# The modulation's sums over partitions: 192 products with a column of ones on TensorE in place of 192 transposes with ScalarE sums

## Chip, cores and metric

The kernel runs on one core of a Trainium2 chip. The metric is the device time of one execution in microseconds. A core has five engines that run side by side, each with a queue that it works through in order: TensorE (PE in the profile, its weight loads PEld), VectorE (DVE), ScalarE (ACT), GpSimd (POOL) and SyncE (SP), which here issues all transfers. Matrix products are written to PSUM, everything else lies in SBUF.

## What is computed

Two layers of a decoder trunk over 256 positions of width 2048, in f32. Each layer has a mixer (sliding-window attention beside RWKV-7 heads) and a SwiGLU FFN. Both are modulated by a vector `mod` that is computed from the condition `c`:

```python
cond = jax.nn.silu(c)                                       # (1, 2048)
for l in range(2):
    mod = (cond @ w_ada[l] + b_ada[l]).reshape(B, 6, 1, 2048)
    sh_m, sc_m, gt_m, sh_f, sc_f, gt_f = [mod[:, i] for i in range(6)]
    u = x * (1 + sc_m) + sh_m
    proj = u @ w_in[l]
    ...
    mix = jnp.concatenate([y_attn, y_rwkv], axis=-1) @ w_out[l]
    x = layer_norm(ALPHA * x + gt_m * mix, ln1_w[l], ln1_b[l])
    u = x * (1 + sc_f) + sh_f
    gate, up = jnp.split(u @ w_gate_up[l], 2, axis=-1)
    x = layer_norm(ALPHA * x + gt_f * ((silu(gate) * up) @ w_down[l]), ln2_w[l], ln2_b[l])
```

The change concerns `cond @ w_ada[l]`, a product of one row with a matrix of 2048 x 12288 in each layer, and of that its last step alone.

## The kernel before

**The weight stream.** The large products (`w_in`, `w_out`, `w_gate_up`, `w_down`) are taken with f32 weights split in two parts. Each piece of 128x1024 is loaded (`raw`), rounded on ScalarE (`hi`, line 380), the rest formed on DVE (`lo`, line 381), and TensorE multiplies three times: lines 402, 403 and 405 where the weights stream, lines 414 to 416 where they are the loaded operand. `raw`, `hi` and `lo` have 4, 3 and 2 buffers.

**The modulation** isn't computed on TensorE. A column of `w_ada` is 2048 long, 16 blocks of 128. For 1024 columns at a time (`ada_steps`, one such piece is called a unit here) 16 tiles `ast` are loaded, and DVE adds them up, each multiplied by its piece of `cond` (lines 255 and 257), into `aacc` (128x1024, one buffer). What is left is a sum over the 128 partitions for each of the 1024 columns: that is `ada_sums`. There are 20 units; they run beside the weight stream from the prologue's end to the second layer's mixer. In the prologue `ada_first` does the same for the first layer's shift and scale in five parts of 4, 4, 2, 4 and 2 blocks, twice each (lines 304 and 306).

**`ada_sums` before.** For each 128 columns TensorE transposes the block of `aacc` into a PSUM bank (line 277), four blocks to a bank. ScalarE copies each transposed block onto itself and adds up along the row with `accum_out` (line 281), which gives 128 sums, one to a partition, as one column of `asum` in SBUF. DVE adds the bias and writes `mods` (line 284). For gates (modulations 2 and 5) a further transpose and a copy bring the row to DRAM (lines 289 to 291).

**Banks.** `bank()` gives out two PSUM banks in turn, `m0` and `m1`, with one buffer each. In the prologue `turn` is set to 0, 0, and all its users (`ada_sums`, the transposes of x at line 354) share one bank: each waits until the one before has been read.

**Order.** The code is written as generators: `pump` and `adv` advance the units between steps of the stream. Then a scheduler orders each engine's instructions by a timeline of its own, so an edit can move instructions that it doesn't touch. On the engines the order is fixed: an instruction that waits holds up all behind it on its engine.

**Two other products** serve for comparison in the prediction. Line 647 sums squares over 64 columns (`kkn`) with two columns of `bones`; line 710 scales `bkc` with a diagonal matrix:

```python
PE.matmul(ssb[0:64, o:o + 2], lhsT=kkn[:, cc * CH:(cc + 1) * CH], rhs=bones[:, 0:P:64], ...)   # 647: 2 x 4 a group of heads
PE.matmul(kb[:, cc * P:(cc + 1) * P], lhsT=bkc[:, cc, :], rhs=s_["de"][:, cc, :], ...)         # 710: 2 x 3 a group of heads
```

There are four groups of heads in each of two layers. `lhsT` is the loaded operand, `rhs` the one that streams. Both are plain f32 products.

Of the kernel before, what the change touches and what calls it, by code (L numbers as in the profile page):

```python
# [10 lines left out]
F32 = mybir.dt.float32  # L11
F32R = mybir.dt.float32r
I32 = mybir.dt.int32
AF = mybir.ActivationFunctionType
ALU = mybir.AluOpType
AX = mybir.AxisListType
# [3 lines left out]
P = 128  # L20
# [24 lines left out]
PARTS = (4, 4, 2, 4, 2)  # L45
LAG = 2
WB = (4, 3, 2)
RED = 1
AR = (3, 7)
AA = (1, 45)  # L50
AP = (0.65, 0.3)
# [16 lines left out]
def hybrid_trunk_kernel(  # L68
# [8 lines left out]
    V, S, G, PE = nc.vector, nc.scalar, nc.gpsimd, nc.tensor  # L77
# [5 lines left out]
    adap = ctx.enter_context(tc.tile_pool(name="adap", bufs=1))  # L83
# [6 lines left out]
    def bank(name="mb", tag="mb"):  # L90

        if tag == "cb":
            return ps.tile([P, 512], F32, tag="cb", name=name)
        t = f"m{turn[0]}"
        turn[0] ^= turn[1]
        return ps.tile([P, 512], F32, tag=t, name=name, bufs=1)


    ident = const.tile([P, P], F32, name="ident")
# [40 lines left out]
    ones = const.tile([P, 1], F32, name="ones")  # L140
# [19 lines left out]
    def prm(l, nm, i, n=1):  # L160
        o = PC[nm] + i
        return par[l][:, o // P, o % P:o % P + n]
# [83 lines left out]
    def ada_steps(l, mod, c0):  # L246

        src = w_ada[l].rearrange("(j p) n -> p j n", p=P)
        n0 = mod * D + c0
        acc = adap.tile([P, 1024], F32, tag="aacc", name="aacc")  # L250
        for j in range(KT):
            t = adap.tile([P, 1024], F32, tag="ast", name="ast", bufs=2)
            dma(t, src[:, j, n0:n0 + 1024])
            if j == 0:
                V.tensor_scalar_mul(acc, t, cond[:, 0:1])
            else:
                ins = V.scalar_tensor_tensor(acc, t, cond[:, j:j + 1], acc, ALU.mult, ALU.add)  # L257
                if anchor:
                    tc.add_manual_dep(ins.ins, anchor[0], order, reason="behind the weight stream")
            yield  # L260
        for _ in range(LAG):
            yield

        ada_sums(l, mod, c0, [acc[:, i * P:(i + 1) * P] for i in range(8)])
        done.add((l, mod, c0 // 1024))
        yield

    def ada_sums(l, mod, c0, blocks):

        col = mod * KT + c0 // P  # L270
        n = len(blocks)
        sm = adap.tile([P, 8], F32, tag="asum", name="asum", bufs=2)
        for q in range(0, n, 4):
            b = bank()
            m = min(4, n - q)
            for i in range(m):
                PE.transpose(b[:, i * P:(i + 1) * P], blocks[q + i], ident)
            for i in range(m):
                bi = b[:, i * P:(i + 1) * P]
                if RED:  # L280
                    S.activation(bi, bi, AF.Copy, accum_out=sm[:, q + i:q + i + 1])
            if not RED:
                V.reduce_sum(sm[:, q:q + m], b[:, 0:m * P].rearrange("p (i k) -> p i k", k=P), axis=AX.X)
        V.scalar_tensor_tensor(mods[l][:, col:col + n], sm[:, 0:n], 1.0 if mod in (1, 4) else 0.0,
                               prm(l, "b_ada", col, n), ALU.add, ALU.add)
        if mod in (2, 5):
            row = adap.tile([8, P], F32, tag="arow", name="arow", bufs=2)[0:n]
            rb = bank()
            PE.transpose(rb[0:n, 0:P], mods[l][:, col:col + n], ident)
            S.copy(row, rb[0:n, 0:P])  # L290
            dma(gates[l, mod // 3, c0 // P:c0 // P + n], row)

    def ada_first(pool, c0, w):

        src = w_ada[0].rearrange("(j p) (m n) -> p j m n", p=P, m=6)
        acc = pool.tile([P, 2, 512], F32, tag="aacc", name="aacc", bufs=2)[:, :, 0:w]
        jj = 512 // w
        for j0 in range(0, KT, jj):
            t = pool.tile([P, jj, 2, w], F32, tag="ast", name="ast", bufs=8)
            for j in range(jj):  # L300
                dma(t[:, j], src[:, j0 + j, 0:2, c0:c0 + w])
            for j in range(jj):
                if j0 + j == 0:
                    V.tensor_scalar_mul(acc, t[:, j], cond[:, 0:1])
                else:
                    V.scalar_tensor_tensor(acc, t[:, j], cond[:, j0 + j:j0 + j + 1], acc, ALU.mult, ALU.add)
            yield
        for m in range(2):
            ada_sums(0, m, c0, [acc[:, m, i * P:(i + 1) * P] for i in range(w // P)])
# [1038 lines left out]
```

## Time and profile before

| | |
|---|---|
| median of 3 runs | 2715.88 us (2715.45 to 2717.28) |
| the profiled execution | 2716.41 us, its span 2714.6 us |
| mean granted TensorE clock | 0.96 |
| read from HBM | 622.08 MB, 234 GB/s over the span |
| aacc steps on DVE (line 257), 300 of 128x1024 | 388.7 us busy, 1296 ns each |
| weight splits on ACT and DVE (lines 380, 381), 728 each | 757.8 us and 885.9 us busy |
| transposes of aacc (line 277) | 192, 31.4 us busy |

Times are in microseconds from the span's start, unless marked ns. "Busy" is the time in which an engine had an instruction running; records of products overlap, so the spacing of their starts tells more than their lengths. In rows of waits stand the waiting instruction, what it waited for, the time in total, how often, and the longest. In rows of the timeline stand the start, the length of the whole group, the engine, the line, the operation, output and inputs, the shapes, and the count; in brackets the idle time of the engine before it and what ended it. The granted clock is TensorE's, 1.00 at full speed.

### The profile page before, as it was taken

The page shows a single profiled execution, that of the slowest core. Times are in us where ns is not written, and L with a number is a line of the kernel's source. Part 1 is how long each engine was busy: PE and PEld are TensorE (multiplying, and loading weights), DVE is VectorE, ACT ScalarE, POOL GpSimd, SP SyncE. Part 2 cuts the span into 40 slices and gives each one's busy share as a digit, 9 for nine tenths or more (in the row PEclk, how much of TensorE's full clock was granted, in tenths as well). Part 3 has the DMA queues.
Part 4 walks back from the last instruction along what each step waited for, and adds up shares of the span by engine and source line. Part 5 has one row for each costly group of instructions (what it writes and reads, how often), then busy time and mean ns, then how long its engine had stood idle before and what let it go on. Part 6 is the DMA issues. An engine that isn't in the chain of part 4 may idle for free. (4 is left out here: it accounts for less than half of the span.)

```text
span 2714.6 us, 41774 instructions
## 1 busy us (share of the span) xinstructions
PE 2517.3 (93%) x15325; PEld 2103.9 (78%) x15325; DVE 1853.5 (68%) x2437; ACT 1188.4 (44%) x2029; POOL 180.0 (7%) x387
## 2 busy tenths in 40 slices
PE   3789998797999999999999989989899999999998
PEld 2787886575788888888889877867788888888887
DVE  6877767879777777777788677565764545545456
ACT  2364452434444444444445544534444444344442
POOL 1002111003000000000000022110120000000000
PEclk9799997798999999999999999979999999999999
DMA  9968667597888888889888586423746655566654
GB/s 310 382 193 254 203 197 225 179 331 250 313 318 308 303 307 304 294 302 309 304 287 288 175 251 204 116 75 130 258 163 190 190 190 190 194 191 189 190 190 148
DMA packets 351999, 637.49 MB, mean 235 GB/s; under 512 B 75894, under 2 KB 142898, under 8 KB 350258
## 3 DMA queue, kind: packets, MB, share of 16 engines
q1 hardware_dynamic: 351794, 634.82, 71.1%
q8 instruction: 120, 1.97, 0.3%
q14 instruction: 85, 0.70, 0.1%
HBM read 622.08 MB, written 12.62 MB: 234 GB/s over the span
## 5 line engine op out<-in xcount | busy, mean ns | idle before, releaser
L380 ACT CAST hi<-raw 128x1024 fp32r<-128x1024 f32 (+2 forms) x728 | 757.8, 1044 | 1097.6 <-PE acc L405 810.6
L381 DVE TENSOR_TENSOR lo<-raw,hi 128x1024 fp32r<-128x1024 f32 (+2 forms) x728 | 885.9, 1220 | 515.8 <-PE acc L403 335.2
L403 PE MATMUL acc<-lo,u 128*128 128x512 f32 x1568 | 515.7, 396 | 16.9 <-DVE lo L381 16.6
L405 PE MATMUL acc<-hi,u 128*128 128x512 f32 x1568 | 507.3, 392 | 0.0
L257 DVE SCALAR_TENSOR_TENSOR aacc<-ast,cond,aacc 128x1024 f32<-128x1024 f32 x300 | 388.7, 1296 | 136.2 <-DMA ast<-in_w_ada_dram 135.1
L402 PE MATMUL acc<-hi,u 128*128 128x512 f32 x1568 | 459.7, 395 | 2.4 <-ACT u L360 1.1
L403 PEld LDWEIGHTS acc<-lo,u 128*128 128x128 f32 x1568 | 294.6, 189 | 83.9 <-DVE lo L381 23.7
L402 PEld LDWEIGHTS acc<-hi,u 128*128 128x128 f32 x1568 | 295.8, 189 | 65.4 <-ACT u L360 1.8
L405 PEld LDWEIGHTS acc<-hi,u 128*128 128x128 f32 x1568 | 296.4, 189 | 62.3 <-issue 0.7
L403 PE MATMUL acc<-lo,ht 128*128 128x512 f32 (+1 forms) x720 | 243.7, 377 | 2.7 <-DVE lo L381 2.6
L405 PE MATMUL acc<-hi,ht 128*128 128x512 f32 (+1 forms) x720 | 242.3, 375 | 0.0
L414 PE MATMUL acc<-u,hi 128*128 128x256 f32 x720 | 206.4, 293 | 12.9 <-ACT hi L380 12.9
L402 PE MATMUL acc<-hi,ht 128*128 128x512 f32 (+1 forms) x720 | 217.1, 376 | 0.0
L415 PE MATMUL acc<-u,hi 128*128 128x256 f32 x720 | 205.6, 292 | 0.0
L416 PE MATMUL acc<-u,lo 128*128 128x256 f32 x720 | 193.7, 295 | 5.3 <-DVE lo L381 5.3
L403 PEld LDWEIGHTS acc<-lo,ht 128*128 128x128 f32 x720 | 135.1, 188 | 28.8 <-DVE lo L381 5.2
L414 PEld LDWEIGHTS acc<-u,hi 128*128 128x128 f32 x720 | 142.8, 199 | 16.7 <-ACT hi L380 13.6
L405 PEld LDWEIGHTS acc<-hi,ht 128*128 128x128 f32 x720 | 135.6, 188 | 24.3
L402 PEld LDWEIGHTS acc<-hi,ht 128*128 128x128 f32 x720 | 134.8, 188 | 24.3
L415 PEld LDWEIGHTS acc<-u,hi 128*128 128x128 f32 x720 | 142.6, 198 | 3.5 <-issue 2.6
L416 PEld LDWEIGHTS acc<-u,lo 128*128 128x128 f32 x720 | 134.4, 198 | 9.5 <-DVE lo L381 6.9
L1067 POOL TENSOR_TENSOR brs<-brs,mhalf 128x1 f32<-128x1 f32 x8 | 5.2, 655 | 1637.3 <-DVE brs L1066 851.5
(349 smaller groups left out, 2950.9 us busy)
## 6 DMA issues: line engine op xcount, KB each, us to landing
ast<-in_w_ada_dram SPq DMA_DIRECT2D x368, 512.0 KB
raw<-in_w_gate_up_dram SPq DMA_DIRECT2D x704, 256.0 KB
raw<-in_w_down_dram SPq DMA_DIRECT2D x176, 512.0 KB
raw<-in_w_in_dram SPq DMA_DIRECT2D x82, 512.0 KB
raw<-in_w_out_dram SPq DMA_DIRECT2D x64, 512.0 KB
raw<-in_w_in_dram SPq DMA_DIRECT2D x120, 256.0 KB
ast<-in_w_ada_dram SPq DMA_DIRECT2D x32, 256.0 KB
lnw<-in_ln_w_dram SPq DMA_DIRECT2D x4, 1024.0 KB
```

The lines of the kernel that those rows point to most:

```text
L257: ins = V.scalar_tensor_tensor(acc, t, cond[:, j:j + 1], acc, ALU.mult, ALU.add)
L380: S.copy(h, fl)
L381: ins = V.tensor_tensor(r, fl, h.bitcast(F32), ALU.subtract)
L402: PE.matmul(bt, lhsT=xh, rhs=hi[:, c0:c0 + w], start=st, stop=False)
L403: PE.matmul(bt, lhsT=xh, rhs=lo[:, c0:c0 + w], start=False, stop=False)
L405: PE.matmul(banks[t][q][:, 0:w], lhsT=xl, rhs=hi[:, c0:c0 + w], start=False, stop=sp_)
L414: PE.matmul(bt, lhsT=hi[:, c0:c0 + w], rhs=xh, start=st and opens, stop=False)
L415: PE.matmul(bt, lhsT=hi[:, c0:c0 + w], rhs=xl, start=False, stop=False)
L416: PE.matmul(bt, lhsT=lo[:, c0:c0 + w], rhs=xh, start=False, stop=sp_ and closes)
L1067: G.tensor_tensor(rs[:, 0:1], rs[:, 0:1], mhalf[:, 0:1], ALU.pow)
```

## The change

The blocks of `aacc` become the loaded operand of a product with a column of ones, `ones` (128x1, set up in the kernel before already). Each product writes 128 sums, one to a partition, as one column of a PSUM bank; eight blocks need one bank and not two. The ScalarE sums and the tile `asum` go, and DVE reads the sums from PSUM.

```diff
-RED = 1
@@ ada_sums
-        sm = adap.tile([P, 8], F32, tag="asum", name="asum", bufs=2)
-        for q in range(0, n, 4):
-            b = bank()
-            m = min(4, n - q)
-            for i in range(m):
-                PE.transpose(b[:, i * P:(i + 1) * P], blocks[q + i], ident)
-            for i in range(m):
-                bi = b[:, i * P:(i + 1) * P]
-                if RED:
-                    S.activation(bi, bi, AF.Copy, accum_out=sm[:, q + i:q + i + 1])
-            if not RED:
-                V.reduce_sum(...)
+        sm = bank()
+        for i in range(n):
+            PE.matmul(sm[:, i:i + 1], lhsT=blocks[i], rhs=ones, start=True, stop=True)
         V.scalar_tensor_tensor(mods[l][:, col:col + n], sm[:, 0:n], 1.0 if mod in (1, 4) else 0.0,
                                prm(l, "b_ada", col, n), ALU.add, ALU.add)
```

ScalarE's 192 copies go; on the other engines every instruction has its counterpart. Lines behind the edit stand 10 lower: the stream's 402, 403 and 405 are 392, 393 and 395, the sums on DVE 274 in place of 284. Because the scheduler orders anew, much moves. Three places follow.

On DVE in the prologue, where the two sums of the second part stand (before, then with the change; `mods` is written by the sum, `aacc` steps belong to the part behind, `lo` to the stream):

```order
L381 TENSOR_TENSOR lo<-raw,hi 128x288
L306 SCALAR_TENSOR_TENSOR aacc<-ast,cond,aacc 128x2x256 x2
L284 SCALAR_TENSOR_TENSOR mods_135<-asum,par_131 128x4
L306 SCALAR_TENSOR_TENSOR aacc<-ast,cond,aacc 128x2x256 x2
L284 SCALAR_TENSOR_TENSOR mods_135<-asum,par_131 128x4
```

```order
L371 TENSOR_TENSOR lo<-raw,hi 128x288
L274 SCALAR_TENSOR_TENSOR mods_135<-mb,par_131 128x4
L296 SCALAR_TENSOR_TENSOR aacc<-ast,cond,aacc 128x2x256 x2
L274 SCALAR_TENSOR_TENSOR mods_135<-mb,par_131 128x4
L296 SCALAR_TENSOR_TENSOR aacc<-ast,cond,aacc 128x2x256 x3
```

Both sums moved two steps ahead; two aacc steps still stand between them.

On PE in the first layer's FFN, around one unit's eight blocks (before, then with the change):

```order
L402 MATMUL acc<-hi,ht 128x512 x4
L277 MATMUL mb<-ident,aacc 128x128 x7
L403 MATMUL acc<-lo,ht 128x512 x2
L405 MATMUL acc<-hi,ht 128x512 x2
L403 MATMUL acc<-lo,ht 128x512 x2
L405 MATMUL acc<-hi,ht 128x512 x2
L402 MATMUL acc<-hi,ht 128x512 x4
L277 MATMUL mb<-ident,aacc 128x128
L403 MATMUL acc<-lo,ht 128x512 x2
```

```order
L392 MATMUL acc<-hi,ht 128x512 x4
L273 MATMUL mb<-ones,aacc 128x1 x4
L393 MATMUL acc<-lo,ht 128x512 x2
L395 MATMUL acc<-hi,ht 128x512 x2
L393 MATMUL acc<-lo,ht 128x512 x2
L395 MATMUL acc<-hi,ht 128x512 x2
L392 MATMUL acc<-hi,ht 128x512 x4
L393 MATMUL acc<-lo,ht 128x512 x2
L395 MATMUL acc<-hi,ht 128x512 x2
L393 MATMUL acc<-lo,ht 128x512 x2
L395 MATMUL acc<-hi,ht 128x512 x2
L392 MATMUL acc<-hi,ht 128x512 x4
```

Seven transposes and one became four products and, directly behind the last row shown, four more; 24 stream products stand between the two halves, where 12 stood.

On PE in the second layer's mixer, where in the profile of before PE waited longest for aacc (before, then with the change; `m` are products of the inversion that the RWKV heads need):

```order
L414 MATMUL acc<-u,hi 128x256
L415 MATMUL acc<-u,hi 128x256
L277 MATMUL mb<-ident,aacc 128x128 x4
L416 MATMUL acc<-u,lo 128x256
L414 MATMUL acc<-u,hi 128x256
L415 MATMUL acc<-u,hi 128x256
L416 MATMUL acc<-u,lo 128x256 x2
```

```order
L404 MATMUL acc<-u,hi 128x256
L405 MATMUL acc<-u,hi 128x256
L273 MATMUL mb<-ones,aacc 128x1 x2
L746 MATMUL m_14526<-tm,yx 64x64 x16
L273 MATMUL mb<-ones,aacc 128x1 x6
L406 MATMUL acc<-u,lo 128x256
L404 MATMUL acc<-u,hi 128x256
```

Four transposes stood together there, four more 16 products later; now two of the unit's products stand ahead of sixteen of the inversion, and the other six right behind these.

More of the change, by code (lines that the diff above doesn't have):

```diff
@@ L271, in ada_sums @@
         n = len(blocks)
-        sm = adap.tile([P, 8], F32, tag="asum", name="asum", bufs=2)
-        for q in range(0, n, 4):
-            b = bank()
-            m = min(4, n - q)
-            for i in range(m):
-                PE.transpose(b[:, i * P:(i + 1) * P], blocks[q + i], ident)
-            for i in range(m):
-                bi = b[:, i * P:(i + 1) * P]
-                if RED:
-                    S.activation(bi, bi, AF.Copy, accum_out=sm[:, q + i:q + i + 1])
-            if not RED:
-                V.reduce_sum(sm[:, q:q + m], b[:, 0:m * P].rearrange("p (i k) -> p i k", k=P), axis=AX.X)
+        sm = bank()
+        for i in range(n):
+            PE.matmul(sm[:, i:i + 1], lhsT=blocks[i], rhs=ones, start=True, stop=True)
         V.scalar_tensor_tensor(mods[l][:, col:col + n], sm[:, 0:n], 1.0 if mod in (1, 4) else 0.0,
```

## The prediction

> **What bounds the kernel now.** I read the page's busy shares first, then the busy time by stage, then who waited for whom, then single stretches of the timeline.
>
> ```profile
> PE 2517.3 (93%) x15325; PEld 2103.9 (78%) x15325; DVE 1853.5 (68%) x2437; ACT 1188.4 (44%) x2029; POOL 180.0 (7%) x387
> ```
>
> TensorE is busy in 93% of the span, ScalarE in 44%. The change takes work from ScalarE and alters work on TensorE, so the question is in which stretches TensorE's time is the span's time. The busy time by stage (start and end; its length; PE; PEld; DVE; ACT; POOL; granted clock; DMA share; GB/s):
>
> ```profile
> 0.00:200.00 200.00, 129.20 (x900) 120.99 (x901) 147.53 (x223) 81.62 (x184) 11.17 (x68) 0.90 0.87 296
> 200.00:400.00 200.00, 192.67 (x1902) 164.41 (x1901) 141.55 (x207) 98.94 (x202) 39.85 (x101) 0.98 0.71 216
> 400.00:720.00 320.00, 261.25 (x1678) 204.69 (x1677) 262.45 (x420) 130.61 (x311) 42.81 (x54) 0.86 0.78 254
> 720.00:1500.00 780.00, 767.64 (x3820) 646.31 (x3818) 598.21 (x610) 354.96 (x537) 2.29 (x5) 1.00 0.88 302
> 1500.00:1760.00 260.00, 247.56 (x2245) 211.22 (x2244) 170.87 (x266) 128.20 (x268) 45.74 (x103) 0.97 0.63 188
> ```
>
> The same stretches for line 277 alone, the transposes that the change replaces (PE, PEld, clock, DMA):
>
> ```profile
> 0.00:200.00 200.00, 6.24 (x32) 4.19 (x32) 0.90 0.87 296
> 200.00:400.00 200.00, 2.24 (x16) 1.83 (x16) 0.98 0.71 216
> 400.00:720.00 320.00, 7.33 (x40) 5.72 (x40) 0.86 0.78 254
> 720.00:1500.00 780.00, 11.00 (x80) 9.48 (x80) 1.00 0.88 302
> 1500.00:1760.00 260.00, 4.60 (x24) 3.37 (x24) 0.97 0.63 188
> ```
>
> These are all 192 (32+16+40+80+24). The 32 in the prologue make ten small units; the other 160 are 20 units of eight. Ten of those lie in 720:1500, where PE is busy for 767.64 of 780 us: what is added to PE there lengthens the span nearly one for one. 200:400 (2 units) and 1500:1760 (3) are 95 to 96% PE. In 400:720 (5 units) PE and DVE have about 262 of 320 us each, and neither is the bound alone.
>
> **What the change takes away.** ScalarE loses 192 copies with their accumulator reads, TensorE 192 transposes:
>
> ```profile
> L281 ACT ACTIVATE mb<-mb x192: 255/262/277, 35.0 to 1753.9; 128x128 f32<-128x128 f32 x192
> L281 ACT ACTIVATION_READ_ACCUMULATOR mb<-mb x192: 180/194/203, 35.1 to 1754.1; 128x1 f32 x192
> L277 PE MATMUL mb<-ident,aacc x192: 270/273/477, 33.7 to 1751.6; 128*128 128x128 f32 x192
> ```
>
> On ScalarE that is at most 192 x (0.262+0.194) = 87.6 us of busy time, on an engine that is idle over half of the span. What a transpose costs the stream is read where eight stand in the middle of it (timeline, PE: start, length, group, count):
>
> ```profile
> 831.83 0.39 PE L405 MATMUL acc<-hi,u 128*128 128x512 f32 x1
> 832.06 1.07 PE L402 MATMUL acc<-hi,u 128*128 128x512 f32 x4
> 832.97 1.03 PE L277 MATMUL mb<-ident,aacc 128*128 128x128 f32 x8
> 833.76 0.71 PE L403 MATMUL acc<-lo,u 128*128 128x512 f32 x2
> ```
>
> Stream products start every (1.07-0.39)/3 = 0.227 us, transposes every (1.03-0.273)/7 = 0.108. The second L403 starts at 833.76+0.71-0.39 = 834.08; without the transposes the two would have started at 832.97 and 833.20. Eight transposes therefore cost **0.88 us**.
>
> **What the change adds.** Each transpose becomes a plain f32 product: the block is the loaded operand (128x128), the column of ones streams (one column). The trace has no such product, but two neighbours:
>
> ```profile
> L710 PE MATMUL kb<-de,bkc x96: 270/275/378, 226.3 to 1781.1; 128*128 128x128 f32 x96
> 226.25 1.50 PE L710 MATMUL kb<-de,bkc 128*128 128x128 f32 x12
> L647 PE MATMUL ssb<-bones,kkn x128: 170/198/219, 181.8 to 1759.2; 128*64 128x2 f32 x128
> 319.05 0.39 PE L402 MATMUL acc<-hi,u 128*128 128x512 f32 x1
> 319.37 0.63 PE L647 MATMUL ssb<-bones,kkn 128*64 128x2 f32 x8
> 319.93 0.49 PE L402 MATMUL acc<-hi,u 128*128 128x512 f32 x1
> ```
>
> First, the counts: the code issues 48 products at L710 and 64 at L647, and the trace has 96 and 128. **A plain f32 product runs as two records, each with its own weight load; a transpose as one** (192 and 192). Second, the spacing: L647, with two streamed columns and 64 loaded ones, is spaced (0.63-0.198)/7 = 0.062 us; L710, with 128 loaded, (1.50-0.275)/11 = 0.111. Two streamed columns can't fill 0.062 us, so L647's spacing is not set by what streams; it goes with the loaded columns, and doubling these about doubles it. For 128 loaded columns and one streamed I take 0.112 a record, L710's, whose loaded shape is the same; the other end is L647's 0.062. A unit is then 16 x 0.112 = 1.79 us (lower end 0.99). At the rims of a narrow group something is lost too: L647's eight push the next L402 from 319.28 to 319.93, 0.65 us, against 8 x 0.062 = 0.50; so 0 to 0.15 a unit, of which I take 0.06. A unit costs 1.85 instead of 0.88: **+0.97 us** (ends +0.11 and +1.06).
>
> The Trainium skill (TensorE: Matmul & The Clock Gate, section LDWEIGHTS) gives a weight load as its column count over 1.2 GHz, whatever the rows: 107 ns for 128 columns and 53 for 64. The measured 0.111 and 0.062 agree; by that rule alone a unit would be 16 x 0.107 = 1.71 us.
>
> By stage, from this execution's 2716.41 us (span 2714.6; the median of three runs is 2715.88, so it stands 0.5 above it):
> - 720:1500: 10 x 0.97 = +9.7.
> - 200:400 and 1500:1760: 5 x 0.97 = +4.9.
> - 400:720: 5 x 0.97 = 4.9, of which I count half, +2.4; all of it if PE ends last there, none if DVE does.
> - Prologue, 32 products: here the chain of latencies matters. Rows of PE for one part:
>
> ```profile
> 80.16 0.60 PE L277 MATMUL mb<-ident,aacc 128*128 128x128 f32 x4
> 82.41 0.66 PE L277 MATMUL mb<-ident,aacc 128*128 128x128 f32 x4 [1.66 <-ACT mb L281]
> 84.94 1.11 PE L354 MATMUL mb<-ident,xt 128*128 128x128 f32 x4 [1.87 <-ACT mb L281]
> 80.79 1.53 DVE L306 SCALAR_TENSOR_TENSOR aacc<-ast,cond,aacc 128x512 f32<-128x512 f32 x2
> 40.00:80.00 40.00, 27.49 (x175) 25.91 (x176) 30.58 (x43) 10.18 (x18) 0.00 (x0) 0.87 0.97 336
> 80.00:110.00 30.00, 21.49 (x152) 19.83 (x151) 25.61 (x44) 15.60 (x42) 0.00 (x0) 0.86 1.07 383
> ```
>
> Now 84.94-80.16 = 4.78 us pass. With the change: eight records and the tail of one, 8 x 0.112 + 0.20 = 1.10, to 81.26; the sum on DVE 0.16, to 81.42; the second four in the shadow of the two aacc steps that stand between the sums in the new order, 1.53, to 82.95; 0.16: 83.11, or 1.8 us earlier. There are three such parts, at 34, 80 and 135. The first two lie where DMA is at 0.97 and 1.07 and PE then waits for weights, so I count nothing for them; the third gives **-1.8**.
> - ScalarE's relief: the weight splits stand behind the sums on its queue.
>
> ```profile
> DVE lo L381 <- ACT mb L281: 2.1, 2, 1.4
> DVE aacc L255 <- PE mb L277: 7.7, 10, 2.2
> ```
>
> All that lo waited for the sums from 200 to 1760 is 2.1 us; PE had products in hand during part of it: **-1.0** (ends 0 and -2.1).
> - The sum on DVE now reads PSUM and holds a bank until it has run. Reading costs nothing by these rows, 162 ns from SBUF and 159 for a similar size from PSUM:
>
> ```profile
> L284 DVE SCALAR_TENSOR_TENSOR mods<-asum,par x30: 152/162/169, 37.2 to 1754.3; 128x8 f32<-128x8 f32 x20, 128x4 f32<-128x4 f32 x6, 128x2 f32<-128x2 f32 x4
> L650 DVE TENSOR_SCALAR rs<-ssb x8: 155/159/167, 198.7 to 1759.4; 64x16 f32<-64x16 f32 x8
> ```
>
> The wait is another thing: DVE stands at the sum until PE's last product is done, and behind it stand lo steps and the next unit's aacc (L255), which waits for that last product too, 7.7 us in ten waits already. The spare stages of raw, hi and lo (4, 3, 2) should cover it in the stream; I take 0 and price the rest below.
>
> Sum: 9.7+4.9+2.4-1.8-1.0 = +14.2, **2730.6 us**.
>
> **Rivals.**
> 1. *Waits that go outweigh the products: faster.* PE stood still in these places of the sums' own chain:
>
> ```profile
> PE mb L277 <- DVE aacc L257: 10.7, 2, 7.3
> PE mb L354 <- ACT mb L281: 6.2, 4, 1.9
> PE mb L277 <- ACT mb L281: 5.8, 3, 2.5
> PE mb L277 <- DVE aacc L306: 4.8, 1, 4.8
> 1608.38 1.28 DVE L257 SCALAR_TENSOR_TENSOR aacc<-ast,cond,aacc 128x1024 f32<-128x1024 f32 x1 [9.17 <-DMA ast<-in_w_ada_dram]
> ```
>
> Together 27.5 us, of which the forecast takes 1.8. If the new order places the products where aacc is ready (one unit of the first mixer stands 17 PE instructions later now) and the prologue keeps its gain, all of it goes: 2730.6-25.7 = 2705. It decides from 9 of the 25.7 us on (within 0.2%) and is faster from 20 on. Against it: the largest wait, 7.3 us, ends with the aacc step at 1608, which itself stood 9.17 us for its transfer; in the new order two of that unit's products still stand ahead of other work (shown with the change), so that wait stays or grows. 0.11.
> 2. *Narrow products are cheap after all.* If the record's spacing has a floor of L647's 0.062 whatever is loaded, PE gets 20 x 0.11 = +2.2, and 2716.4+2.2-1.8-1.0 = 2715.8: no change. For it: no row has 128 loaded columns with one streamed. Against it: the doubling from L647 to L710. 0.13. The skill's same page (section Wait — 56ns, not 53.3ns?) puts the floor at about 25 ns however narrow; by that a unit would be 0.40 us and the time some 2704; no run here shows such spacing between equal tiles.
> 3. *DVE stalls at the sums: slower still.* Where lo has no spare stage, the mixers and the layer's end (400:720 and 1500:1760, 8 units), each unit holds DVE for up to the 1.8 us of its products and PE waits for lo after it: 8 x 1.8 = +14, 2745. It decides where DVE reaches the sum before PE's last product, as when the products are moved behind stream work and the sum is not (one unit of the first layer's output projection stands 22 PE instructions later, its sum at the same place). 0.14.
>
> **How the numbers follow.** Forecast 0.62, rivals 0.11, 0.13, 0.14. The forecast's own ends: 20 x 1.06 = 21.2 with no relief and no prologue gain, 2737.6; with 400:720 free, the prologue's waits on ACT gone (12.0) and 2.1 of relief, 2716.4+14.6-14.1 = 2717. The range reaches half-way into the rivals: **2709 to 2743**. Measurement tells about 0.2% (5.4 us) from no change: faster is rival 1 and the low tail of 2, 0.15; same is most of 2 and the forecast's lowest end, 0.16; slower 0.69.
>
> **What would show it.** In the profile after: 384 records for the new products, spaced 0.112 (step 1 wrong at 0.06); PE busy in 720:1500 up by about 9.7 with that stretch longer by as much; PE's waits on ACT sums gone in the prologue; DVE's waits at the sum small in the stream. The prediction fails if the order of the mixers shifts waits by more than 10 us, which no row of before can price.

## The result, and the profile after

The changed kernel takes 2741.20 us (median of 5 runs, 2739.94 to 2744.56) against 2715.88 for the kernel before: ratio 1.0095, 95% interval 1.0081 to 1.011. It is 0.95% slower; the medians lie 25.3 us apart, where 14.2 were forecast. The profiled execution took 2742.8 us, its span 2740.7, which is 26.1 over the span before. Its busy times on the page, and then by stage with the columns of the prediction's table:

```profile
PE 2544.3 (93%) x15517; PEld 2130.9 (78%) x15517; DVE 1849.2 (67%) x2437; ACT 1126.0 (41%) x1645; POOL 189.8 (7%) x387
```

```profile
0.00:200.00 200.00, 139.35 (x994) 132.05 (x995) 151.63 (x230) 72.77 (x122) 12.18 (x68) 0.89 0.88 303
200.00:400.00 200.00, 189.34 (x1791) 161.88 (x1792) 136.28 (x196) 87.74 (x162) 41.52 (x101) 0.96 0.69 214
400.00:720.00 320.00, 259.40 (x1739) 205.76 (x1738) 252.10 (x416) 117.00 (x233) 45.57 (x54) 0.85 0.72 240
720.00:1500.00 780.00, 767.74 (x3764) 642.33 (x3763) 587.11 (x595) 322.37 (x365) 2.75 (x5) 1.00 0.86 297
1500.00:1760.00 260.00, 243.18 (x2234) 210.30 (x2233) 172.29 (x265) 115.91 (x213) 44.75 (x102) 0.96 0.64 195
```

ScalarE loses 62 us of busy time and TensorE gains 27. In 720:1500 TensorE is as busy as before, 767.74 of 780 us: what the new products add there can only make the stretch longer. The new products' row, and one unit of eight in the stream (timeline: start, length, group, count):

```profile
L273 PE MATMUL mb<-ones,aacc x384: 164/250/373, 33.7 to 1753.3; 128*128 128x1 f32 x192
```

```profile
784.22 1.07 PE L392 MATMUL acc<-hi,u 128*128 128x512 f32 x4
785.13 1.84 PE L273 MATMUL mb<-ones,aacc 128*128 128x1 f32 x16
786.83 0.72 PE L393 MATMUL acc<-lo,u 128*128 128x512 f32 x2
```

192 products make 384 records. The second L393 starts at 786.83+0.72-0.39 = 787.16; without the unit it would have been 785.36. A unit costs 1.80 us, 0.112 a record, where eight transposes cost 0.88: +0.92, forecast +0.97. Who waited for whom on PE, and on DVE at the sum:

```profile
PE acc L393 <- DVE lo L371: 25.5, 29, 3.7
PE acc L896 <- DVE qr L889: 19.7, 3, 18.4
PE m L739 <- DVE ytr L735: 17.7, 3, 7.9
PE mb L273 <- DVE aacc L296: 6.5, 2, 6.0
PE mb L273 <- DVE mods L274: 2.6, 3, 1.5
PE mb L344 <- DVE mods L274: 1.5, 4, 0.7
...
PE mb L273 <- DVE aacc L256: 0.2, 1, 0.2
```

```profile
DVE mods L274 <- PE mb L273: 12.5, 13, 2.2
```

And before, for qr on PE and at the sum on DVE:

```profile
PE acc L906 <- DVE qr L899: 11.3, 4, 5.7
```

```profile
DVE mods L284 <- ACT mb L281: 11.4, 11, 2.0
```

The waits for ScalarE's sums (6.2 and 5.8) and for aacc in the units (10.7) are gone or 0.2. New is one wait of **18.4 us for qr**, the rotated queries of the attention; before, the longest of that kind was 5.7. DVE's stand at the sums isn't new: it stood 11.4 us for ScalarE's sums before, and stands 12.5 for the products now.

Where the time went is read by matching the weight stream's products (the third line of each kind, 405 and 416 before) one by one and taking the difference of their starts, changed less before, at a few places in the time of before. Each row is one profiled execution; the last column is the difference of the spans.

```
at (us of before)            195    420    560    720   1500   1960   2700   span
the change                  -4.8   +5.3  +12.3   +9.9  +25.2  +23.6  +26.1  +26.1
e5  the change again        -4.6   +5.1  +19.0  +17.5  +28.7  +22.9  +25.0  +25.1
e1  order of before         -4.7   -1.3   +4.8   +8.0  +27.5  +35.1  +38.7  +38.7
e2  no products             -7.9   +2.4  +10.4   +8.2  +15.1   +7.4  +11.1  +11.1
e3  mixer as before         -5.1   -1.9   -0.3   -0.9  +10.9   +9.0  +13.0  +13.1
e4  one record              -4.4   +9.1  +17.1  +15.9  +22.2  +16.7  +19.3  +19.4
e6  e2 and e3 together      -8.2   -8.3   -9.8  -11.1   -7.9  -14.2  -10.7  -10.6
e7  e4 and e3 together      -6.1   -5.4   -5.5   -6.7   -2.3   -6.2   -4.4   -4.3
e8  products in prologue    -3.4   -3.9   -4.1   -4.5   -4.5   -4.1   -1.7   -1.7
e9  430 to 470 as before    -6.4   -0.0   -2.2   -3.0  +10.7   +5.3   +9.8   +9.8
e10 mixer but 430 to 470    -7.3   -5.1  +15.1  +14.1  +25.2  +24.1  +32.3  +32.4
e11 e1, sums later          -4.6   -0.4   +2.8   +4.8  +30.4  +40.6  +43.0  +43.0
e12 e1, products early      -1.8   -0.9   +9.1   +9.2  +20.3  +27.6  +29.3  +29.4
```

The second row is another execution of the changed kernel (e5, below). It lies up to 7.6 us off the first at one place, so a difference of a few us between two single rows shows little.

In its first execution the change gains 4.8 us in the prologue, loses 17 in the first mixer (195 to 560), 15.3 in 720:1500, and little after that. The first mixer's loss is not made of products alone: a stand on SP precedes it. SP's rows of it after and before (timeline; a start is that of the first issue of a group):

```profile
434.56 1.31 SPq L717 DMA_DIRECT2D nb<-nscr  x2
448.07 1.54 SPq L728 DMA_DIRECT2D tinv<-ttl  x2
451.22 1.27 SPq L731 DMA_DIRECT2D tm<-tinv  x2
452.53 4.59 SPq L252 DMA_DIRECT2D ast<-in_w_ada_dram  x2
457.22 0.39 SPq L878 DMA_DIRECT2D qk<-qkv  x1
```

```profile
433.69 3.99 SPq L253 DMA_DIRECT2D ast<-in_w_ada_dram  x2
442.58 0.38 SPq L888 DMA_DIRECT2D qk<-qkv  x1
...
450.34 1.28 SPq L738 DMA_DIRECT2D tinv<-ttl  x2
...
456.78 1.28 SPq L741 DMA_DIRECT2D tm<-tinv  x2
```

And DVE and PE of the change at the same place:

```profile
454.88 0.71 DVE L735 STREAM_TRANSPOSE ytr<-tm 128x512 f32<-128x512 f32 x1 [14.53 <-DMA tm<-tinv]
```

```profile
464.56 0.47 PE L896 MATMUL acc<-ident,qr 128*128 128x128 f32 x1 [18.36 <-DVE qr L889]
```

Before, SP loaded qk first and stored POOL's inverse afterwards. Now the store of `tinv` stands ahead: SP stands from 436 to 448 for POOL, which writes `ttl` until 448, DVE stands 14.5 us at `ytr` for what comes of it, and the load of qk and its rotation stand behind, 15 us later than before. This suggested that the loss there came with the order and not with the products.

### The profile page after: what moved, and what is told of

It is laid out like the page before. It is cut to its first block, busy times and chain, and to the rows that moved or that the text cites. A ratio compares the mean times of both kernels' runs of the same rounds, so it can differ in the third digit from the quotient of the medians.

```text
span 2740.7 us, 41786 instructions
## 1 busy us (share of the span) xinstructions
PE 2544.3 (93%) x15517; PEld 2130.9 (78%) x15517; DVE 1849.2 (67%) x2437; ACT 1126.0 (41%) x1645; POOL 189.8 (7%) x387
## 4 chain that ended last, share of the span: by engine, by line
PE 75%; DMA 11%; DVE 7%; POOL 2%; issue 2%; ACT 1%; SPq 1%; DVEq 0%; POOLq 0%; ACTq 0%
PE acc L393 19%; PE acc L395 19%; PE acc L392 19%; DMA ast<-in_w_ada_dram 5%; PE acc L406 2%; PE acc L405 2%; PE acc L404 2%; DVE lo L371 2%; DVE aacc L256 2%; DMA raw<-in_w_gate_up_dram 2%; DMA raw<-in_w_in_dram 1%; POOL tmp L723 1%; PE mb L273 1%; POOL ttl L725 1%; PE aa L674 1%
## 5 line engine op out<-in xcount | busy, mean ns | idle before, releaser
L393 PE MATMUL acc<-lo,u 128*128 128x512 f32 x1568 | 518.8, 397 | 21.4 <-DVE lo L371 21.3
L393 PEld LDWEIGHTS acc<-lo,u 128*128 128x128 f32 x1568 | 294.1, 189 | 91.9 <-DVE lo L371 32.3
L393 PE MATMUL acc<-lo,ht 128*128 128x512 f32 (+1 forms) x720 | 244.6, 379 | 2.4 <-DVE lo L371 2.4
L393 PEld LDWEIGHTS acc<-lo,ht 128*128 128x128 f32 x720 | 134.8, 188 | 30.2 <-DVE lo L371 4.9
```

Of the source, the lines that this page charges most:

```text
L393: PE.matmul(bt, lhsT=xh, rhs=lo[:, c0:c0 + w], start=False, stop=False)
```

## Experiments

An order was held by adding, at the end of the program, issue-order dependences between the instructions of an engine; what is left out of them ("loose") the scheduler places.

```diff
+LOOSE = set()
+def pin(nc, tc):
...
+        for a, b in zip(place[:-1].tolist(), place[1:].tolist()):
+            tc.add_manual_dep(ins[b], ins[a].name, free, reason="pinned order")
...
         hybrid_trunk_kernel(tc, *args)
+        pin(nc, tc)
```

Each run is compared with the kernel before, timed on the same chip. The figure behind each median is the distance from before in us with its 95% interval, both taken from the ratio of the runs ("by the ratio"); the distance of the two medians can differ from it by some us. One profiled execution, as in the table above, can lie several us off the median.

### One of the two suspects at a time: e1 to e4

**e1**, the change in the order of before, products and sums loose:

```diff
-            PE.matmul(sm[:, i:i + 1], lhsT=blocks[i], rhs=ones, start=True, stop=True)
+            LOOSE.add(PE.matmul(sm[:, i:i + 1], lhsT=blocks[i], rhs=ones, start=True, stop=True).ins.name)
...
```

> The change, but every other instruction of all five engines is held to the order of before; only the 192 products and the 30 sums on DVE find their own places. Theory (products and order): the change costs 20 units x 0.92 = 18.4 us on TensorE, gains about 4.8 in the prologue, and the rest of the measured +25.3, some 12 us, is the new order; so here 2716 + 18.4 - 4.8 = 2729.5, within 3. Rival 1 (no order: the sum on DVE that waits for the products, and the bank that it holds, stall what is behind them wherever they stand): 2741, as the change. Rival 2 (all order, the products cost nothing that lasts): 2711 to 2716.

**e2**, the change's own order, without products:

```diff
-            PE.matmul(sm[:, i:i + 1], lhsT=blocks[i], rhs=ones, start=True, stop=True)
+            PE.transpose(sm[:, i % 4 * P:(i % 4 + 1) * P], blocks[i], ident)
```

> The change in its own order, held on all engines, but each product is a transpose of the block into the same bank again (one record in place of two); the sums over partitions are left out, so the modulation isn't the reference's. Theory: TensorE gets 20 x 0.92 = 18.4 us back, and the order's loss stays: 2741.2 - 18.4 = 2723, within 3. Rival 1 (stalls at the sum on DVE): these shrink too, so 2723 or less, and DVE's wait for the products goes from 12.5 us to about half. Rival 2 (all order): 2741.

**e3**, the change's order, except that what before issues from 195 to 555 us is held in the order of before (products and sums loose):

> The change in its own order, except that in the first layer's mixer (195 to 555 us of before) all but the products and their sums stand in the order of before. Theory: the mixer's loss of about 12 us goes, the products' 18.4 stay: 2741.2 - 11.5 = 2730, within 3, and PE's wait of 18.4 us for qr is gone. Rival 1 (stalls at the sums): 2741. Rival 2 (all order, spread over all stages): 2730 to 2736.

**e4**, one record a product instead of two:

```diff
-        acc = adap.tile([P, 1024], F32, tag="aacc", name="aacc")
+        acc = adap.tile([P, 1024], F32R, tag="aacc", name="aacc")
...
-            PE.matmul(sm[:, i:i + 1], lhsT=blocks[i], rhs=ones, start=True, stop=True)
+            PE.matmul(sm[:, 2 * i:2 * i + 2], lhsT=blocks[i], rhs=ones_r, start=True, stop=True)
```

> The change in its own order, but aacc and the column of ones are fp32r (aacc is rounded to it at every step), with two equal columns of ones, so that a product should be one record as the stream's are. Theory (cost is two records of one weight load each): 192 records, spaced 0.11 us, a unit 0.90 in place of 1.81: 2741.2 - 18 = 2723, as with the transposes. Rival (cost is a matter of the narrow output, not of the records): 2741.

Measured, in this order: 2754.94 us (+39, 34 to 44 by the ratio), 2727.33 (+13, 8 to 17), 2736.69 (+21, 14 to 27), 2737.59 (+24, 18 to 30).

- e1 fell outside all that was expected: the old order, with the products where the scheduler put them, is worse than the change's. Why is taken up with e11 and e12.
- e2: the products are worth about half; the time, 13 us over before, misses the theory's 2723, which is 7 over. In the table e2 and the change part by 3.1 us up to 195, by 8.4 in 720:1500 and by 6.1 in 1500:1960, and not at all in the first mixer, where PE stands for qr with or without them (19.7 us at the longest in e2). Against the change's second row they part by 4.3 in 720:1500, 1.9 in 1500:1960 and 6.0 from 195 to 720. DVE's stand at the sums fell to 5.7 us, the sign named for rival 1; so e2 takes away two things at once, TensorE's time for the products and what DVE stands for them.
- e3: in the profile the first mixer's loss is gone (-0.3 at 560). The time is less clear: the four runs spread from 2729 to 2739 us, and their median lies above the 2727 to 2733 of the theory.
- e4: the theory's time was missed. In the stream the step was right (its lines stand 2 lower):

```profile
L275 PE MATMUL mb<-ones_r,aacc x192: 164/250/371, 33.3 to 1745.7; 128*128 128x2 f32 x192
```

```profile
788.10 1.07 PE L394 MATMUL acc<-hi,u 128*128 128x512 f32 x4
789.01 0.95 PE L275 MATMUL mb<-ones_r,aacc 128*128 128x2 f32 x8
789.82 0.72 PE L395 MATMUL acc<-lo,u 128*128 128x512 f32 x2
```

192 records, a unit for 790.15-789.23 = 0.92 us, nearly as cheap as transposes. In the profile 720:1500 lost 6.3 us, where the change's two rows lost 15.3 and 11.2. But the first mixer cost 21 us there, in the change's order, and took part of the gain back. That the median fell by so little is not explained by this alone.

### Both together, and the prologue alone: e5 to e8

**e5** is the change itself, **e6** is e2's edit in e3's order, **e7** e4's edit in e3's order. **e8** is the kernel before in its own order, with products only in `ada_first`:

```diff
-        sm = adap.tile([P, 8], F32, tag="asum", name="asum", bufs=2)
-        for q in range(0, n, 4):
+        if first:
+            sm = bank()
+            for i in range(n):
+                LOOSE.add(PE.matmul(sm[:, i:i + 1], lhsT=blocks[i], rhs=ones, start=True, stop=True).ins.name)
+        else:
+            sm = adap.tile([P, 8], F32, tag="asum", name="asum", bufs=2)
+        for q in range(0, 0 if first else n, 4):
```

> The change as it is, timed beside the three others here, so that their distances can be taken on one chip. Both theories: 25 us over the kernel before (21 to 29 us).

> The change with its two suspected costs taken away together: transposes of 0.113 us stand where the products stood (the ScalarE sums stay out, so this leaves out the sums over partitions), and the first mixer (195 to 555 us) is held to the order of before. Theory (products' PE time about 14 us, the order of the first mixer about 12 us, nothing else of size): the time comes back to that of before, -3 to +3 us. Rival (the engines' order outside the first mixer, or the lighter ScalarE stream, costs of its own): 8 us or more over before remains.

> The one-record product (aacc and the ones rounded to fp32r, two columns of ones) in the change's order, with the first mixer held to the order of before. Theory: with half the records the products cost no more than the transposes did, so this stands where the run without products and with before's mixer stands, -3 to +5 us beside before; the miss of the earlier one-record run came from the first mixer alone (17 us late at its end). Rival: rounding aacc or the one-record product has a price outside the mixer, and 12 us or more over before remains.

> Products with ones only for the eight sums of the prologue, everything else as in the kernel before (transposes and ScalarE sums) and in its order. Theory: the change's gain is in the prologue (its stream is 5 to 6 us ahead there), its losses all come later; the gain stays in part, so 2 to 6 us faster than before. Rival (the prologue ends with the arrival of the weights and what is gained there is waited for in the first mixer): within 1 us of before.

Measured: 2741.74 us (+30, 25 to 36); 2708.34 (-4.6, -8.7 to -0.5); 2721.76 (+9, 5 to 13); 2715.71 (+2, -1 to +5).

- e5 is the change, 27 us over before by the medians and 30 by the ratio.
- e6 came out a little below the forecast: with products and mixer order both taken away, all of the loss is gone and a small gain is left. In the table it lies in the prologue (-8.2) and in the second mixer (-6.3 from 1500 to 1960). e6 leaves the sums out, so it isn't a kernel to use; it shows that even sums that cost TensorE no more than the transposes would bring some 5 us in this order, 9 at most by the interval.
- e3 less e6, the same order with and without products, is 23.7 us in the profiles and 25 by the ratio. Of that 8.6 lie in 720:1500, as with e2, and 7.1 in 195:720, where the change's own order hid them. Both changes together (26.1 + 10.6 = 36.7 in the profiles) take more than the two single ones added up (15.0 and 13.0), for the most part for that reason.
- e7: theory's window was -3 to +5, its rival's 12 and more; the median lies between, the profile (the fastest of ten) inside the theory's. Against e3, which has the same order and two records (+21), the one-record product removes most of the price; that it removes all is not shown.
- e8: the lead of the prologue is there in the profile until 1960, but no gain can be told in the time. The theory's 2 to 6 us are not confirmed, and the rival's "within 1 us of before" lies inside the interval.

### Which piece of the order: e9 and e10

**e9** holds only what before issues between 430 and 470 us to the order of before. SP's difference from the change:

```
-L717 DMA nb<-nscr 64x16x16 x2
-L728 DMA tinv_154<-ttl 64x8x16 x2
-L731 DMA tm<-tinv_154 64x8x64 x2
...
 L878 DMA qk<-qkv 128x2x256
...
 L878 DMA qk<-qkv 128x2x256
 L879 DMA qk<-qkv 128x2x64
+L728 DMA tinv_154<-ttl 64x8x16 x2
...
+L731 DMA tm<-tinv_154 64x8x64 x2
```

> The change in its own order, with only what the kernel before issues between 430 and 470 us put back into the order of before, on all engines: SP loads qk ahead of the stores of tinv and tm, and DVE rotates q (qr) ahead of ytr. Products, and what DVE sums behind them, are loose. Theory (the first mixer's loss is PE's wait of 18.4 us for qr, because SP stands for ttl and DVE for tm ahead of qr): that wait shrinks to under 6 us, and the time is 8 to 13 us under the change's, 2728 to 2733 us, or 12 to 18 us beside before. Rival (the loss is spread over 200 to 430 us, where the change lost 8 us of its lead): within 4 us of the change, 23 to 27 us over before.

**e10** holds the rest of the first mixer to the order of before, and leaves this stretch in the change's.

> The complement: the first mixer (195 to 555 us) in the order of before except the stretch from 430 to 470 us, which keeps the change's order. Theory (the stretch holds the loss): PE's long wait for qr stays at 15 us or more, and 20 to 27 us over before. Rival (spread over the rest of the mixer): 10 to 16 us over before, and the wait is short.

Measured: 2733.91 us (+22, 15 to 29) and 2745.24 (+31, 24 to 37). PE's wait for qr in e9, then in e10:

```profile
PE acc L896 <- DVE qr L889: 3.2, 3, 1.8
```

```profile
PE acc L896 <- DVE qr L889: 18.4, 3, 17.1
```

The wait goes with these 40 us of order and stays without them, and in the table the loss of 420 to 560 goes and stays with it (-2.2 and +20.2). So the place is shown. Its worth in time is smaller than in the profiles, where e9 lies 16 us under the change: the eight runs of e3 and e9 lie 20.3 us over before on average, the thirteen of the change, e5 and e10, where the stretch is the change's, 27.9, with a standard error of some 2 us on the difference. The lowest of the thirteen is 24.1, and five of the eight lie under it. I take 8 us, in single executions up to 16. Taken alone the times decide less: e9 (22) lies between the theory's 12 to 18 and the rival's 23 to 27, and the 6 us lost from 195 to 420 are still in it; e10 (31) lies above its theory's 20 to 27.

Which engine's rows do it, SP's, DVE's or another's, was not tried apart and stays open.

### Why the old order was worse: e11 and e12

In e1 DVE stood long at the sum, for products that came late, and PE then ran out of split weights. DVE's stand in all of e1, then one such place on DVE and on PE:

```profile
DVE mods L274 <- PE mb L273: 48.3, 17, 7.3
```

```profile
850.85 0.17 DVE L274 SCALAR_TENSOR_TENSOR mods<-mb,par 128x8 f32<-128x8 f32 x1 [6.36 <-PE mb L273]
850.93 0.75 DVE L254 TENSOR_SCALAR aacc<-ast,cond 128x1024 f32<-128x1024 f32 x1
851.60 1.22 DVE L371 TENSOR_TENSOR lo<-raw,hi 128x1024 fp32r<-128x1024 f32 x1
```

```profile
850.54 0.28 PE L273 MATMUL mb<-ones,aacc 128*128 128x1 f32 x2
852.88 1.00 PE L393 MATMUL acc<-lo,u 128*128 128x512 f32 x2 [2.06 <-DVE lo L371]
853.67 1.05 PE L395 MATMUL acc<-hi,u 128*128 128x512 f32 x2
```

**e11** moves the sums of nine units, and the writes of aacc behind them, later on DVE. At one of them (in the order of DVE, `-` e1, `+` e11):

```
+L371 TENSOR_TENSOR lo<-raw,hi 128x1024 x3
 L274 SCALAR_TENSOR_TENSOR mods<-mb,par 128x8
 L254 TENSOR_SCALAR aacc<-ast,cond 128x1024
-L371 TENSOR_TENSOR lo<-raw,hi 128x1024 x3
```

> The run in the order of before (41 us over it), with one thing changed: where DVE stood over 0.9 us at a sum for its products, the sum and the writes of aacc behind it (which wait for the same products) come one to four splits lo later on DVE. Theory (PE runs dry because DVE stands at the sum with the next lo behind it, and the clock is cut after each such stop, as the stops at 850 and 1216 us show): PE's waits for lo between 720 and 1500 us fall from 9.7 to under 6 us, the jumps of 4.7 and 4.2 us go, and the time is 8 to 14 us less, 27 to 33 us over before. Rival (the stops come from the split itself or the order, not from the sum): 37 to 43 us over before.

**e12** leaves the order of before as it is and holds the products and the sums of 29 of the 30 units to the places of the transposes and sums of before.

> The order of before on every engine again, but with the products held to the places on TensorE where the transposes stood, and the sums on VectorE to theirs (one unit of thirty, in the second mixer, stays loose); in the earlier run in the order of before both were loose, and DVE stood 48.3 us for products that came late. Theory (that run's 41 us came from late products: the sum and aacc's next write wait for them on DVE, and SP stands for aacc with the weight loads behind it, 31.1 us between 720 and 1500 us): DVE's stand for the products falls under 15 us, SP's for aacc under 10 us, PE's waits for lo in that stretch under 6 us, and the time is 8 to 18 us over before, about the products' own price. Rival (an order made for the old code costs the new one 35 us by itself, wherever the products stand): 33 us or more over before.

Measured: 2761.20 us (+46, 41 to 52) and 2744.24 (+25, 20 to 31). What SP waited for aacc between 720 and 1500 us in e1, e11 and e12:

```profile
SPq L252 <- DVE aacc L254: 31.1, 8, 7.2
```

```profile
SPq L252 <- DVE aacc L254: 35.0, 6, 9.9
```

```profile
SPq L252 <- DVE aacc L254: 7.5, 5, 1.6
```

And what PE waited for lo in that stretch in e11, and in e12 (there line 398 is the 393 of the others):

```profile
PE acc L393 <- DVE lo L371: 10.0, 12, 1.7
```

```profile
PE acc L398 <- DVE lo L376: 3.5, 7, 0.9
```

e11 took most of DVE's stand away (48.3 to 9.9 us in all), and the time did not fall (46 against 39, with intervals that overlap): that theory fell as it was stated, and the time lies above the rival's 37 to 43 as well. What e11 had left was SP. aacc has one buffer, its next write waits for the late products, `ast` isn't freed, and SP stands at the next `ast` load with the weight loads behind it. In e12, with the products early, DVE's stand at the sums falls to 7.9 us, SP's to 7.5, PE's to 3.5, as its theory said, the loss in 720:1500 from 19.5 to 11.1, and the time by 14 us (by the ratio, each beside its own before; 9 in the profiles). So late products cost 9 to 14 of e1's 39 us, by way of DVE and of SP; the two were not separated.

e12 stays above the theory's 8 to 18, and at +25 it is no better than the change: the old order as a whole, with the products in the transposes' places, is not cheap for the new code either. Of the 10.0 us that its profile loses in 420:560, 5.3 lie between the two products that stand at 536 and 550 us before. That stretch in before, then in e12 (clock in the third column from the end):

```profile
536.00:550.00 14.00, 10.83 (x47) 8.53 (x46) 11.76 (x18) 7.97 (x26) 0.00 (x0) 0.88 0.75 228
```

```profile
539.80:559.10 19.30, 15.70 (x55) 12.93 (x54) 11.91 (x18) 5.60 (x10) 0.00 (x0) 0.65 0.70 224
```

PE's longest wait there is 3.2 us in before and 3.6 in e12, but the granted clock is 0.65 in place of 0.88: an estimate from these rows, length times clock, makes both stretches equally long at full clock (12.3 and 12.5 us). The other half, and the 7 us in 1500:1960, are not explained.

## Why the prediction came out as it did

The sign was right, the time lies in the range, and the size was 11 us short. That it lies in the range is in part luck: the forecast's own upper end was 2737.6, and the room above it, up to 2743, was made for rival 3, of which little came; another loss filled it. By its own steps, with the change's first row of the table:

- **The price of a unit**: +0.97 forecast, +0.92 measured; 384 records, 0.112 each. Rival 2 (a floor of 0.062) is out. The Trainium skill (TensorE: Matmul & The Clock Gate, section LDWEIGHTS) gives 107 ns for a load of 128 columns. This row agrees with it; L647's 0.062 stood further off its 53 ns for 64 columns. The same page of the Trainium skill (section Wait — 56ns, not 53.3ns?) has a floor of some 25 ns for narrow products. It is not what spaces these records, which stand 112 ns apart.
- **720:1500**: +9.7 forecast. The five executions that have the products and the change's order there (the change, e5, e3, e9, e10) lost 15.3, 11.2, 11.8, 13.7 and 11.1 us, 12.6 on average; the two without products (e2, e6) lost 6.9 and 3.2. So the products cost about 8 (8.4 and 8.6 in the two closest pairs), near the 10 x 0.92 = 9.2 of their time on TensorE, and some 5 us are lost in the change's order without products too. A part may be more waits for lo (7.0 us, 4.2 before); the rest is open.
- **200:400 and 400:720**, +1.9 and +2.4: this is **the step that failed**. It priced the products in waits that it took to stay as they were. From 195 to 720 the change lost 14.7 us (22.1 in e5), and e2 lost 16.1 without products: a price of the products can't be told there. The new order put SP's store and DVE's `ytr` ahead of the attention's rotation, and PE stood 18.4 us. With the old order the same products do cost 7.1 there (e3 against e6). The prediction named this as what would make it fail, more than 10 us by the order of the mixers, and gave it neither a term nor a rival.
- **1500:1760**, +2.9 for three units: against e2 the products cost 6.1 up to 1960 in the change and 1.9 in e5, but the stretch as a whole got 1.6 and 5.8 shorter. PE's wait of 7.3 us for aacc, which was to stay or grow, went: this part of rival 1 came true. The relief of ScalarE was put at 1.0 in all; e6 gains 6.3 us in this stretch, in which its order has a part too.
- **The prologue**: -1.8 forecast, -4.8 measured (-7.9 and -8.2 without products). In the second part the chain of two sums runs from the first product to line 344:

```profile
77.02 1.02 PE L273 MATMUL mb<-ones,aacc 128*128 128x1 f32 x8 [0.48 <-DVE aacc L296]
78.73 1.25 PE L273 MATMUL mb<-ones,aacc 128*128 128x1 f32 x8 [0.69 <-DVE mods L274]
80.32 1.11 PE L344 MATMUL mb<-ident,xt 128*128 128x128 f32 x4 [0.34 <-DVE mods L274]
```

  It takes 3.30 us now and took 4.78 before, so 1.5 less. The forecast gave its gain to the third part and nothing to the first two; but the lead was 4.8 us at 91 us already (3.4 in e5), ahead of the third. e8 has a lead of 3.4 in its profile, and no gain in its time.
- **Rival 3**, DVE stands at the sum: 12.5 us in the change, hardly more than the 11.4 it stood for ScalarE before. The prediction counted the new stand and not the old one; PE's waits for lo (L393) came to 25.5 us, 22.1 before (L403). In e1 it came true with 48.3 us, through lo and through SP and aacc's one buffer.

So the 26.1 us of the profiled execution are: the prologue -4.8, the first mixer up to 720 us +14.7, for the most part by its order, the ten units of the stream +8.4, other losses there +6.9, the rest +0.9. In e5 the prologue has -4.6, the first mixer +22.1, 720:1500 +11.2 and the rest -3.6: the places are the same, but their shares are known to several us only. No kernel that was run and computes the sums is faster than the kernel before.

## What to carry to other kernels

Moving work from an idle engine to the one that sets the time pays only for waits that it ends; here even sums at no extra cost would have ended some 5 us of them. Where a scheduler places instructions, an edit also buys a new order of everything: compare the orders of SP and DVE in the stages with long chains, and run the edit with the order held, before the edit itself gets the blame. A held order is no neutral ground, though: with the products loose in it they came late (e1), and with the products in the old places it cost as much as the new order (e12). When a producer comes late, look past the engine that waits for it: here the stand went on through a single buffer to the queue that loads the weights.

## What was not expected of the hardware

A short stop of TensorE can cost nearly twice its length. In e1 PE stands 2.06 us at 850.8, and the pairs of products behind it take 1.00 to 1.05 us in place of 0.62. Windows of 2 us there (clock in the third column from the end):

```profile
850.00:852.00 2.00, 0.81 (x6) 0.61 (x4) 1.15 (x3) 0.88 (x1) 0.00 (x0) 1.00 0.00 0
852.00:854.00 2.00, 1.12 (x3) 0.95 (x4) 2.00 (x4) 0.00 (x0) 0.00 (x0) 0.79 0.63 164
854.00:856.00 2.00, 2.00 (x6) 1.51 (x6) 0.43 (x2) 0.00 (x0) 0.00 (x0) 0.50 0.89 286
856.00:858.00 2.00, 2.00 (x9) 1.59 (x8) 0.90 (x1) 1.05 (x1) 0.00 (x0) 0.86 0.93 325
```

The granted clock falls to 0.50 and is back after some 4 us. The stream stood at +11.2 against before ahead of the stop and at +15.3 from 857.8 us on; 0.2 of this is the product of two records in between, so the stop cost 3.8. The same stop of 2.06 us at 1216 us took the stream from +20.7 to +25.0, 3.8 without the four records there.

Not every such stop does this. Where PE waits 1.83 us for `vx`, the clock fell to 0.50 in the change and stayed at 1.00 in e1. The stop ends at 1522.61 us in the change and at 1525.76 in e1, and the rows behind it are, in this order:

```profile
1524.00:1526.00 2.00, 2.00 (x10) 2.00 (x11) 0.45 (x2) 0.00 (x0) 0.00 (x0) 0.50 0.35 124
```

```profile
1526.00:1528.00 2.00, 2.00 (x14) 1.48 (x13) 1.60 (x5) 0.47 (x1) 0.00 (x0) 1.00 0.87 262
```

So equal waits can have different prices, and single executions of one kernel differ: e3's four runs took 2729.4, 2734.1, 2739.2 and 2739.5 us at a mean granted clock of 0.962, 0.957, 0.955 and 0.954.
